# One more pair of contraction tiles by seven products in the key and value projections, another order of the first query block, and another order of the fold's splits

## The chip, the cores and the metric

The kernel runs on one core of a Trainium2 chip. The metric is the device time of one execution in microseconds (us). It is given as the median of the runs; beside it stands one execution that was profiled, with its span from the first to the last instruction. PE is the tensor engine, DVE the vector engine, ACT the scalar engine, and SP issues the transfers of the weights.

## The reference, cut to what matters

One encoder layer over 256 tokens of 2048 channels, in float32: a feed-forward half step, a mixer, attention over 256 memory tokens, a second feed-forward half step, and a last norm. The change lies in the attention:

```python
x = x + mem_cross_attention(rms_norm(x, xattn_norm), rms_norm(mem, mem_norm), w_q, w_kv, w_o)

def mem_cross_attention(h, mem_h, w_q, w_kv, w_o):      # 4 heads of 512
    q = (h @ w_q).reshape(b, s, 4, 512)
    kv = (mem_h @ w_kv).reshape(b, 256, 2, 4, 512)
    k, v = kv[:, :, 0], kv[:, :, 1]
    logits = jnp.einsum('bshd,bmhd->bhsm', q, k) * 512 ** -0.5
    p = jax.nn.softmax(logits, axis=-1)
    o = jnp.einsum('bhsm,bmhd->bshd', p, v).reshape(b, s, 2048)
    return o @ w_o
```

## The kernel before, in words

**Products in two parts.** Every float32 operand is split into a high part, which ACT casts, and a low part, which DVE gets as the difference to the high part. One product of two operands is then three matmuls: high by high, high by low, low by high. Weights come from HBM in units of 1 MB (two contraction tiles of 128 rows by 1024 columns) into one of three buffers `raw`; a unit's high and low parts are `wh` and `wl`. The units are numbered through the whole program; in the instruction orders below `wl185` belongs to unit 185. A profile's rows leave the numbers out.

**Plain units and units of 7.** A block (`block_s`) multiplies 256 rows of activations `xs` by 1024 columns of weights in 8 units. A plain unit is 8 products, 24 matmuls of 512 columns. In a unit of 7 (`split_seven`, `seven`) the two tiles of rows and the two of columns are taken as a 2 by 2 product with 7 products in place of 8, 21 matmuls. It needs sums of the weights and of the activations. DVE makes the weights' sums in `T` (three additions, L445), ACT casts the high parts of the sums (`wh`, two casts, L448) and of the raw columns (`xh`, L261), and DVE subtracts for `wl` (L449) and `xl` (L262). A plain unit has one ACT cast (L261) and one DVE subtraction (L262). The sums of the activations are made once for each pair of contraction tiles (`Sums.make`): an addition (L406) and four small ones (L413 to L418) on DVE, with a split of the results into `ye` and back into `xs` (L267 on ACT, L268 on DVE).

**Order.** `Stream` writes the work unit by unit: weights are split two units ahead of the unit that PE multiplies, and a raw buffer is loaded again once its unit is split. Splits of weights stand on ACT and DVE in the order in which they are written (`in_turn`), sums of activations among them (`among_weights`). `st.op(f, n)` puts other work behind the n-th next unit. A scheduler then sets each engine's order at build time; on the chip each engine runs its own instructions strictly in order.

**Buffers of the attention.** `T`, `xh` and `xl` have no tiles of their own here: they take turns in tiles of the attention stage that are free (`KV_HOMES`). In the key and value blocks `xh` and `xl` together have two tiles of one name, `att`. So a unit of 7 can cast its `xh` only when the previous unit of 7 has made its last product with the tile that is taken over.

**The stage.** Two query blocks (`w_q`), then key block 0, value block 0, key block 1, value block 1 (`w_kv`). The query blocks are units 182 to 189 and 190 to 197, the key and value blocks 198 to 229 in eights. Before the query blocks `fold` turns x by PE transposes into a PSUM tile of two banks, four pieces of 256 columns, and splits each piece into `xs` (`split_scaled`: ACT L230, then DVE L231). `mem_fold` does the same with the memory tokens, in place of x, once the second query block no longer needs those pairs. After a block its four extra products are combined (L530 to L535) and joined (L545). The queries and keys of a head are turned (L735); `logits` (L1273) with the softmax and `probs` follow a key block, `values` (L1312) a value block.

Before, the query blocks have the pairs 4 and 5 as units of 7, the key and value blocks the pairs 0 and 4.

Of the kernel before, what the change touches and what calls it, by code (L numbers as in the profile page):

```python
# [15 lines left out]
D = 2048  # L16
S = 256
# [3 lines left out]
NB = 512  # L21
# [9 lines left out]
G_FFN1, G_MIX, G_X, G_MEM, G_FFN2, G_PS, G_HN, G_BA, G_END = 0, 16, 32, 48, 64, 80, 88, 96, 100  # L31
# [62 lines left out]
def build(ctx, tc, I, out):  # L94
# [36 lines left out]
    def ptile(name):  # L131
        return psum.tile([P, 2, NB], F32, tag="ps", name=name)

    def four(ps):
        return ps.rearrange("p a (b c) -> p (a b) c", c=S)
# [3 lines left out]
    def uid(s):  # L139
        cnt[0] += 1  # L140
        return f"{s}{cnt[0]}"
# [42 lines left out]
    xs = main.tile([P, KT, 2, S], F32R, tag="xs", name="xs")  # L184
    ys = main.tile([P, KT, 2, S], F32R, tag="ys", name="ys")

    def gcol(i):
        return gains[:, i : i + 1]
# [4 lines left out]
    def f32(ap):  # L193
        return ap.bitcast(F32)
# [30 lines left out]
    def spread(ps, t, d):  # L225

        nc.tensor.matmul(ps[:, t * P : (t + 1) * P], ones, d, start=True, stop=True)

    def split_scaled(dst, kt, src, scale):
        hi = nc.scalar.activation(dst[:, kt, 0, :], src, AF.Copy, scale=scale)  # L230
        lo = nc.vector.scalar_tensor_tensor(  # L231
            out=dst[:, kt, 1, :], in0=src, scalar=scale, in1=f32(dst[:, kt, 0, :]),
            op0=ALU.mult, op1=ALU.subtract,
        )
        return hi, lo
# [16 lines left out]
    def among_weights(f):  # L252


        scalar, vector = behind_weights(f)
        latest["vector"] = vector
        if scalar is not None:
            latest["scalar"] = scalar
# [7 lines left out]
    def split(hi, lo, src):  # L266
        high = nc.scalar.copy(hi, src)  # L267
        return high, nc.vector.tensor_tensor(out=lo, in0=src, in1=f32(hi), op=ALU.subtract)  # L268
# [10 lines left out]
    diag, rows = {}, {}  # L279
# [301 lines left out]
    def wload(dst, w, k0, n, n0, cols=NB):  # L581
        nc.sync.dma_start(
            dst, w[k0 * P : (k0 + n) * P, n0 : n0 + cols].rearrange("(k p) n -> p k n", p=P)
        )
# [9 lines left out]
    def wwide(w, n0, k0=0, nk=KT):  # L594

        def src(k):
            def load(raw):
                raw = raw.rearrange("p (k n) -> p k n", n=2 * NB)
                if len(loaded) < 3:
                    for kk in range(2):  # L600
                        parts = (0, NB) if not loaded else (0,)
                        for c in parts:
                            n = 2 * NB // len(parts)
                            wload(raw[:, kk : kk + 1, c : c + n], w, k + kk, 1, n0 + c, n)
                else:
                    wload(raw, w, k, 2, n0, 2 * NB)
                next(first_loads, None)
                loaded.append(1)
            return load
        return [src(k0 + k) for k in range(0, nk, 2)]  # L610
# [51 lines left out]
    def x_cols(c, n):  # L662

        b = c // (2 * NB)
        return xrows[b][:, :, c - b * 2 * NB : c - b * 2 * NB + n]

    def x_chunk(c):
        v = ptile(uid("px"))[:, 0, :].rearrange("p (a b) -> p a b", a=2)
        k = 2 * c
        for j in range(2):  # L670
            for h in range(2):
                nc.tensor.transpose(
                    v[:, j, h * P : (h + 1) * P], x_cols((k + j) * P, P)[:, h], ident
                )
        for j in range(2):
            rows["parts", c, j] = split_scaled(xs, k + j, v[:, j, :], gcol(G_FFN1 + k + j))
        if c:
            latest["scalar"], latest["vector"] = rows["parts", c, 1]

# [60 lines left out]
    def fold(c, gain):  # L740

        v = four(ptile(uid("px")))
        x = x_cols(c * NB, NB)
        for j in range(4):
            for h in range(2):
                nc.tensor.transpose(  # L746
                    v[:, j, h * P : (h + 1) * P], x[:, h, j * P : (j + 1) * P], ident
                )
        def parts():
            for j in range(4):  # L750
                done = split_scaled(xs, 4 * c + j, v[:, j, :], gcol(gain + 4 * c + j))
            return done

        among_weights(parts) if c >= 2 else parts()
        for h in range(2):
            q = tmp.tile([P, NB], F32, tag="j", name=uid("j"))
            nc.scalar.activation(q, x[:, h], AF.Square, accum_out=ss[:, h, c : c + 1])
# [429 lines left out]
    def homes(of):  # L1187
        return lambda: scope.update(shared={tag: list(of[tag]) for tag in of})
# [7 lines left out]
    def xt(name, shape, dt=F32, tag=None, bufs=1):  # L1196
        t = whole_lines(scope["pool"], shape, dt, tag or name, uid(name), bufs)
        xa[name] = t
        return t
# [16 lines left out]
    def mem_fold(c):  # L1216

        v = four(ptile(uid("tm")))
        for j in range(4):
            for h in range(2):  # L1220
                nc.tensor.transpose(
                    v[:, j, h * P : (h + 1) * P],
                    xa[f"mem{h}"][:, c * NB + j * P : c * NB + (j + 1) * P], ident,
                )
        for j in range(4):
            split_scaled(xs, 4 * c + j, v[:, j, :], gcol(G_MEM + 4 * c + j))

    OUTPUT.make_sums((1, 4))
# [3 lines left out]
    for c in range(4):  # L1232
# [4 lines left out]
    w_q, w_kv, w_o = I["xattn_w_q"][0], I["xattn_w_kv"][0], I["xattn_w_o"][0]  # L1237


    q_sums, Q_ORDER = Sums("ye", xs, (4, 5), True, 2), ((0, 1, 2, 4, 3, 5, 6, 7),  # L1240
                                                        (0, 1, 4, 2, 5, 3, 6, 7))
    kv_sums, KV_ORDER = Sums("ye", xs, (0, 4), True, 2), (1, 5, 2, 0, 3, 6, 4, 7)
    held = {}

    def ev_Q(b):
        def evict(j, c):
            for h in range(2):
                nc.scalar.activation(c[:, h, :], c[:, h, :], AF.Copy, scale=Rcol[:, h : h + 1])
            held["Q", b, j] = c
        return evict  # L1250

    def turn_Q(b, j):
        k = 8 * b + 4 * j
        split(ys[:, k : k + 4, 0, :], ys[:, k : k + 4, 1, :], rows_turned(held["Q", b, j]))

    def turn_K(h):
        v = rows_turned(held["K", h])
        K = xa["K", h] = xt("K", [P, 4, 2, M], F32R, tag="kv", bufs=2)
        split(K[:, :, 0, :], K[:, :, 1, :], v)

    def ev_V(b):
        def evict(j, c):
            V = xa["V", 2 * b + j] = xt("V", [P, 2, 2, XHD], F32R, tag="kv", bufs=2)
            split(V[:, :, 0, :], V[:, :, 1, :], c)
        return evict
# [25 lines left out]
    def probs(h):  # L1291
        ps = ptile(uid("pt"))
        for mtile in range(2):
            for t in range(2):
                nc.tensor.transpose(
                    ps[:, mtile, t * P : (t + 1) * P], xa["P", h][:, t, mtile * P : (mtile + 1) * P], ident
                )
        if h % 2 == 0:
            xt("PT", [P, D], F32R)
        PT = xa["PT", h] = xa["PT"][:, h % 2 * 4 * S : (h % 2 + 1) * 4 * S].rearrange(  # L1300
            "p (m a s) -> p m a s", m=2, a=2
        )
        split(PT[:, :, 0, :], PT[:, :, 1, :], ps[:, :, :S])
# [11 lines left out]
                    )  # L1315
            split_pair(ys, 4 * h + 2 * p, ps[:, :, :S])

    for g, after in zip(q_sums.pairs, (2, 4)):
        st.op(lambda g=g: among_weights(lambda: q_sums.make(g)), after)
    for b in range(2):  # L1320
        block_s(wwide(w_q, b * 2 * NB), xs, q_sums, Q_ORDER[b], ev_Q(b))
        for j in (1, 0):
            st.op(lambda b=b, j=j: turn_Q(b, j), 1)
        if b == 0:
            for c, after in enumerate((5, 7, 6, 8)):
                st.op(lambda c=c: mem_fold(c), after)
    st.op(homes(KV_HOMES))
    for g, after in zip(kv_sums.pairs, (0, 2)):
        st.op(lambda g=g: among_weights(lambda: kv_sums.make(g)), after)
    for b in range(2):  # L1330
        block_s(wwide(w_kv, b * 2 * NB), xs, kv_sums, KV_ORDER, lambda j, c, b=b: held.__setitem__(
            ("K", 2 * b + j), c))
        for j in (1, 0):
            h = 2 * b + j
            st.op(lambda h=h: turn_K(h), 1)
        for h in (2 * b, 2 * b + 1):
            st.op(lambda h=h: logits(h), 2)
            st.op(lambda h=h: probs(h), 3)
        block_s(wwide(w_kv, D + b * 2 * NB), xs, kv_sums, KV_ORDER, ev_V(b))
        for h in (2 * b, 2 * b + 1):  # L1340
            st.op(lambda h=h: values(h), 1)
    st.op(homes(OUT_HOMES))
# [214 lines left out]
```

## Time and profile before

| | |
|---|---|
| median of 3 runs | 2091.51 us (2090.76 to 2091.64) |
| the profiled execution | 2093.45 us, span 2091.6 us |
| PE busy | 2075.2 us, 99% of the span |
| DVE, ACT busy | 1795.8 us (86%), 1134.2 us (54%) |
| read from HBM | 417.58 MB, 208 GB/s over the span |

The profiled execution is 1.94 us longer than the median; 1.85 us of it lie around the span. Matmuls overlap in the record: one lasts 390 ns from start to end, but the next starts earlier than that, so PE counts as busy while it is waiting for less than the overlap. A wait of PE is therefore best seen in the starts of its rows.

### The profile page before, as it was taken

What the parts mean: (1) busy time and instruction counts of PE and PEld (TensorE: products, weight loads), DVE (VectorE), ACT (ScalarE), POOL (GpSimd) and SP (SyncE); (2) the same over time, 40 slices, a digit from 0 to 9 for tenths busy, and PEclk for the clock granted to TensorE, in tenths of its full rate; (3) what the DMA queues carried; (4) which work ended last, traced back from release to release, by engine and by line L of the source; (5) the groups of instructions that cost most, each with busy time, mean ns of one, the idle gap of its engine ahead of it and who ended that gap; (6) DMA issues with size and microseconds to landing.
All of it is one profiled execution on the core that took longest, in us unless ns stands there. A gap on an engine that the chain in (4) does not pass through costs nothing.

```text
span 2091.6 us, 24183 instructions
## 1 busy us (share of the span) xinstructions
PE 2075.2 (99%) x9669; PEld 1728.6 (83%) x9669; DVE 1795.8 (86%) x1639; ACT 1134.2 (54%) x1118; POOL 14.2 (1%) x41
## 2 busy tenths in 40 slices
PE   9999999999999999999999999999999999999998
PEld 7888888888888888888788888888888888888886
DVE  7999899989998677688788777879998999989974
ACT  7655455644654555365665544556554556545544
POOL 0000000000000000000000000000000000000001
PEclk9999999999999999999999999999999999999999
DMA  7556666566656655467555555656576765676673
GB/s 263 201 196 228 240 221 207 194 223 237 226 195 239 215 181 192 152 198 264 198 185 185 174 182 174 222 189 220 181 241 209 243 207 187 224 239 223 209 255 118
DMA packets 131321, 435.94 MB, mean 208 GB/s; under 512 B 9860, under 2 KB 13544, under 8 KB 130824
## 3 DMA queue, kind: packets, MB, share of 16 engines
q1 hardware_dynamic: 131176, 434.38, 61.2%
q8 instruction: 76, 1.25, 0.2%
q14 instruction: 37, 0.30, 0.0%
q10 hardware_dynamic: 32, 0.01, 0.0%
HBM read 417.58 MB, written 16.78 MB: 208 GB/s over the span
## 4 chain that ended last, share of the span: by engine, by line
PE 93%; DVE 3%; ACT 1%; issue 1%; DMA 1%; SPq 0%; DVEq 0%; ACTq 0%
PE pt L344 53%; PE pt L468 25%; PE pa L329 6%; PE pe L344 3%; PE pb L344 2%; PE ph L735 1%; DVE wl L262 1%; DVE T L445 1%; DVE wl L449 1%; PE pl L1273 1%; PE pv L1312 1%; ACT wh L261 0%; PE px L746 0%; DVE xl L262 0%; DMA raw<-in_xattn_w_kv 0%
## 5 line engine op out<-in xcount | busy, mean ns | idle before, releaser
L262 DVE TENSOR_TENSOR wl<-raw,wh 128x2048 fp32r<-128x2048 f32 (+2 forms) x267 | 597.9, 2246 | 146.7 <-ACT wh L261 145.7
L344 PE MATMUL pt<-wh,xs 128*128 128x512 f32 x2112 | 677.9, 390 | 0.0
L261 ACT CAST wh<-raw 128x2048 fp32r<-128x2048 f32 (+2 forms) x267 | 500.3, 1879 | 289.4 <-PE pt L344 120.9
L344 PEld LDWEIGHTS pt<-wh,xs 128*128 128x128 f32 x2112 | 395.6, 188 | 81.0
L448 ACT CAST wh<-T 128x1024 fp32r<-128x1024 f32 x230 | 241.8, 1053 | 361.1 <-DVE T L445 355.0
L344 PE MATMUL pt<-wh,ys 128*128 128x512 f32 x1360 | 427.9, 390 | 0.0
L344 PE MATMUL pt<-wl,xs 128*128 128x512 f32 x1056 | 412.7, 391 | 0.0
L344 PEld LDWEIGHTS pt<-wh,ys 128*128 128x128 f32 x1360 | 254.9, 188 | 52.5
L344 PE MATMUL pt<-wl,ys 128*128 128x512 f32 x680 | 264.9, 390 | 0.0
L449 DVE TENSOR_TENSOR wl<-T,wh 128x2048 fp32r<-128x2048 f32 x115 | 262.6, 2283 | 1.2 <-ACT wh L448 0.5
L344 PEld LDWEIGHTS pt<-wl,xs 128*128 128x128 f32 x1056 | 198.4, 188 | 41.2 <-DVE wl L262 0.5
L262 DVE TENSOR_TENSOR xl<-raw,xh 128x1536 fp32r<-128x1536 f32 x115 | 201.3, 1751 | 18.9 <-ACT xh L261 17.3
L261 ACT CAST xh<-raw 128x1536 fp32r<-128x1536 f32 x115 | 170.1, 1479 | 32.3 <-PE pt L468 20.3
L445 DVE TENSOR_TENSOR T<-T,raw 128x512 f32<-128x512 f32 x230 | 158.7, 690 | 6.1
L344 PEld LDWEIGHTS pt<-wl,ys 128*128 128x128 f32 x680 | 127.7, 188 | 26.3
L468 PE MATMUL pt<-wh,xs 128*128 128x512 f32 x368 | 143.5, 390 | 0.7 <-ACT xs L267 0.7
L445 DVE TENSOR_TENSOR T<-raw 128x1024 f32<-128x1024 f32 x115 | 140.0, 1218 | 0.5
L468 PE MATMUL pt<-xh,xs 128*128 128x512 f32 x368 | 138.2, 391 | 0.1
L329 PE MATMUL pa<-xs,wh 128*128 128x512 f32 x384 | 135.0, 396 | 0.0
L468 PE MATMUL pt<-wh,xe 128*128 128x512 f32 x320 | 124.5, 389 | 0.0
L329 PE MATMUL pa<-xs,wl 128*128 128x256 f32 x384 | 106.6, 281 | 0.0
L329 PEld LDWEIGHTS pa<-xs,wh 128*128 128x128 f32 x384 | 71.7, 188 | 16.0 <-issue 0.3
(237 smaller groups left out, 2304.0 us busy)
## 6 DMA issues: line engine op xcount, KB each, us to landing
raw<-in_ffn_w_down SPq DMA_DIRECT2D x88, 1024.0 KB, 5.5
raw<-in_ffn_w_up SPq DMA_DIRECT2D x80, 1024.0 KB, 5.0
raw<-in_ffn_w_gate SPq DMA_DIRECT2D x77, 1024.0 KB, 5.2
raw<-in_w_in SPq DMA_DIRECT2D x32, 1024.0 KB, 5.2
raw<-in_xattn_w_kv SPq DMA_DIRECT2D x32, 1024.0 KB, 5.1
raw<-in_w_out SPq DMA_DIRECT2D x16, 1024.0 KB, 5.6
raw<-in_xattn_w_q SPq DMA_DIRECT2D x16, 1024.0 KB, 5.8
raw<-in_xattn_w_o SPq DMA_DIRECT2D x16, 1024.0 KB, 5.6
```

Of the source, the lines that this page charges most:

```text
L261: in_turn("scalar", lambda: nc.scalar.copy(hi, src))
L262: in_turn("vector", lambda: nc.vector.tensor_tensor(out=lo, in0=src, in1=f32(hi), op=ALU.subtract))
L329: nc.tensor.matmul(o, w, x, start=k == 0 and i == 0, stop=last and i == 1)
L344: nc.tensor.matmul(ps, a, w, start=first and i == 0, stop=last and i == 2)
L445: in_turn("vector", lambda: nc.vector.tensor_tensor(out=o, in0=a, in1=b, op=ALU.add))
L448: in_turn("scalar", lambda: nc.scalar.copy(th[:, c], t[:, c]))
L449: in_turn("vector", lambda: nc.vector.tensor_tensor(out=tl, in0=t, in1=f32(th), op=ALU.subtract))
L468: nc.tensor.matmul(banks[n], x, w, start=n in fresh and j == 0, stop=n in ends and j == 2)
L735: nc.tensor.transpose(v[:, i, h * P : (h + 1) * P], g[:, h, i * P : (i + 1) * P], ident)
L1273: nc.tensor.matmul(ps[:, t, :M], ys[:, 4 * h + d, a, tok], xa["K", h][:, d, b, :], start=i == 0, stop=i == 11,)
L1312: nc.tensor.matmul(ps[:, d, :S], xa["V", h][:, m, a, col], xa["PT", h][:, m, b, :], start=i == 0, stop=i == 5,)
```

## The change

1. The four pieces of a folded tile are split in the order 0, 2, 1, 3 in place of 0, 1, 2, 3 (`BY_BANKS`), so that neighbours lie in different PSUM banks; the first feed-forward's `x_chunk` puts its two pieces into two banks.
2. The first query block runs its pairs in natural order: the pairs 4 and 5, its units of 7, stand fifth and sixth (before: fourth and sixth). Their sums are made behind units 3 and 4 (before: 2 and 4).
3. The keys and values get a third pair of 7, pair 3. Key block 0 runs its pairs as 1, 5, 2, **0**, 6, **3**, **4**, 7 and the three other blocks as 1, 5, **0**, 2, **3**, 6, **4**, 7 (units of 7 bold; before: 1, 5, 2, **0**, 3, 6, **4**, 7 in all four). The last `mem_fold` comes one unit later. Pair 4's sums get a tile of their own, `ye2`.

```diff
+    BY_BANKS = (0, 2, 1, 3)
...
     def x_chunk(c):
-        v = ptile(uid("px"))[:, 0, :].rearrange("p (a b) -> p a b", a=2)
+        v = ptile(uid("px"))
...
-            rows["parts", c, j] = split_scaled(xs, k + j, v[:, j, :], gcol(G_FFN1 + k + j))
+            rows["parts", c, j] = split_scaled(xs, k + j, v[:, j, :S], gcol(G_FFN1 + k + j))
...
         def parts():
-            for j in range(4):
+            for j in BY_BANKS:
                 done = split_scaled(xs, 4 * c + j, v[:, j, :], gcol(gain + 4 * c + j))
...
-        for j in range(4):
+        for j in BY_BANKS:
             split_scaled(xs, 4 * c + j, v[:, j, :], gcol(G_MEM + 4 * c + j))
...
-    q_sums, Q_ORDER = Sums("ye", xs, (4, 5), True, 2), ((0, 1, 2, 4, 3, 5, 6, 7),
+    q_sums, Q_ORDER = Sums("ye", xs, (4, 5), True, 2), ((0, 1, 2, 3, 4, 5, 6, 7),
                                                         (0, 1, 4, 2, 5, 3, 6, 7))
-    kv_sums, KV_ORDER = Sums("ye", xs, (0, 4), True, 2), (1, 5, 2, 0, 3, 6, 4, 7)
+    kv_sums = Sums("ye", xs, (0, 3, 4), True, 2)
+    KV_ORDER = ((1, 5, 2, 0, 6, 3, 4, 7), (1, 5, 0, 2, 3, 6, 4, 7))
...
-    for g, after in zip(q_sums.pairs, (2, 4)):
+    for g, after in zip(q_sums.pairs, (3, 4)):
...
-            for c, after in enumerate((5, 7, 6, 8)):
+            for c, after in enumerate((5, 7, 6, 9)):
                 st.op(lambda c=c: mem_fold(c), after)
...
-    for g, after in zip(kv_sums.pairs, (0, 2)):
+    for g, after in zip(kv_sums.pairs, (0, 3, 4)):
...
-        block_s(wwide(w_kv, b * 2 * NB), xs, kv_sums, KV_ORDER, lambda j, c, b=b: held.__setitem__(
+        block_s(wwide(w_kv, b * 2 * NB), xs, kv_sums, KV_ORDER[b], lambda j, c, b=b: held.__setitem__(
...
-        block_s(wwide(w_kv, D + b * 2 * NB), xs, kv_sums, KV_ORDER, ev_V(b))
+        block_s(wwide(w_kv, D + b * 2 * NB), xs, kv_sums, KV_ORDER[1], ev_V(b))
```

The order of SP's transfers and of POOL's work is the same in both programs, and so is that of the other engines outside the attention. Lines behind the first edit are 3 or 4 higher: L262 is L265, L468 is L471. In the folds every ACT split of a tile but its first waits for the DVE split just ahead of it, before and after alike; only the pieces' numbers differ.

How the instructions move is shown at three places. First DVE in the first query block, from the end of the fold on. Before, unit 185 is the first unit of 7, with a plain unit between it and the second, 187:

```order
L445 TENSOR_TENSOR T185_7409<-raw185_7275 128x1024
L445 TENSOR_TENSOR T185_7409<-T185_7409,raw185_7275 128x512 x2
L262 TENSOR_TENSOR xl185_7413<-raw185_7275,xh185_7412 128x1536
L449 TENSOR_TENSOR wl185_7411<-T185_7409,wh185_7410 128x2048
L406 TENSOR_TENSOR j282_7460<-xs_107 128x512
L413 TENSOR_TENSOR j282_7460<-j282_7460 128x128
L414 TENSOR_TENSOR j282_7460<-j282_7460 128x128
L415 SCALAR_TENSOR_TENSOR j282_7460<-j282_7460 128x128
L268 TENSOR_TENSOR xs_107<-j282_7460,xs_107 128x128
L418 TENSOR_TENSOR j282_7460<-j282_7460 128x128
L262 TENSOR_TENSOR wl186_7471<-raw186_7305,wh186_7470 128x2048
L445 TENSOR_TENSOR T187_7508<-raw187_7339 128x1024
```

The same place after:

```order
L265 TENSOR_TENSOR wl185_7410<-raw185_7275,wh185_7409 128x2048
L448 TENSOR_TENSOR T186_7450<-raw186_7305 128x1024
L448 TENSOR_TENSOR T186_7450<-T186_7450,raw186_7305 128x512 x2
L265 TENSOR_TENSOR xl186_7454<-raw186_7305,xh186_7453 128x1536
L452 TENSOR_TENSOR wl186_7452<-T186_7450,wh186_7451 128x2048
L409 TENSOR_TENSOR j286_7498<-xs_107 128x512
L416 TENSOR_TENSOR j286_7498<-j286_7498 128x128
L417 TENSOR_TENSOR j286_7498<-j286_7498 128x128
L271 TENSOR_TENSOR xs_107<-j286_7498,xs_107 128x128
L418 SCALAR_TENSOR_TENSOR j286_7498<-j286_7498 128x128
L421 TENSOR_TENSOR j286_7498<-j286_7498 128x128
L448 TENSOR_TENSOR T187_7508<-raw187_7339 128x1024
```

The plain unit's subtraction stands first now, the two units of 7 (186, 187) follow each other, and the same instructions stand behind the fold in both.

Second, DVE at the end of key block 0. Before, unit 203 is plain and unit 204 is the next unit of 7 after 201:

```order
L262 TENSOR_TENSOR wl203_8219<-raw203_8089,wh203_8218 128x2048
L445 TENSOR_TENSOR T204_8247<-raw204_8152 128x1024
L268 TENSOR_TENSOR ye314_8074<-j320_8178,ye314_8074 128x384
L268 TENSOR_TENSOR ys_108<-ph318_8117,ys_108 128x4x256
L268 TENSOR_TENSOR ys_108<-ph319_8128,ys_108 128x4x256
L445 TENSOR_TENSOR T204_8247<-T204_8247,raw204_8152 128x512 x2
L262 TENSOR_TENSOR xl204_8251<-raw204_8152,xh204_8250 128x1536
L449 TENSOR_TENSOR wl204_8249<-T204_8247,wh204_8248 128x2048
```

After, units 203 and 204 are both of 7:

```order
L452 TENSOR_TENSOR wl203_8220<-T203_8218,wh203_8219 128x2048
L409 TENSOR_TENSOR j324_8257<-xs_107 128x512
L416 TENSOR_TENSOR j324_8257<-j324_8257 128x128
L417 TENSOR_TENSOR j324_8257<-j324_8257 128x128
L271 TENSOR_TENSOR xs_107<-j324_8257,xs_107 128x128
L418 SCALAR_TENSOR_TENSOR j324_8257<-j324_8257 128x128
L421 TENSOR_TENSOR j324_8257<-j324_8257 128x128
L448 TENSOR_TENSOR T204_8267<-raw204_8152 128x1024
L271 TENSOR_TENSOR ye2323_8256<-j324_8257,ye2323_8256 128x384
L448 TENSOR_TENSOR T204_8267<-T204_8267,raw204_8152 128x512 x2
L265 TENSOR_TENSOR xl204_8271<-raw204_8152,xh204_8270 128x1536
L452 TENSOR_TENSOR wl204_8269<-T204_8267,wh204_8268 128x2048
```

Pair 4's sums and the additions for `T204` stand behind `wl203` now, where `T204` stood ahead of unit 204's turn before.

Third, PE in value block 0, where the delayed products of one unit of 7 end and those of the next begin. Before (units 209 and 212; two plain stretches of unit 211 and six more products of 209 follow ahead of unit 212's first):

```order
L468 MATMUL pt341_8596<-xh209_8439,xs_107 128x512
L468 MATMUL pt341_8596<-xl209_8440,xs_107 128x512
L468 MATMUL pt341_8596<-xh209_8439,xs_107 128x512
L468 MATMUL pt341_8596<-wh209_8437,ye314_8074 128x512
L468 MATMUL pt341_8596<-wl209_8438,ye314_8074 128x512
L468 MATMUL pt341_8596<-wh209_8437,ye314_8074 128x512
L344 MATMUL pt325_8387<-wh211_8590,xs_107 128x512 x2
L344 MATMUL pt325_8387<-wl211_8591,xs_107 128x512
```

After (units 208 and 210; `pl336` are the logits of a head):

```order
L1277 MATMUL pl336_8527<-K329_8447,ys_108 128x256 x24
L471 MATMUL pt340_8577<-xh208_8400,xs_107 128x512
L471 MATMUL pt340_8577<-xl208_8401,xs_107 128x512
L471 MATMUL pt340_8577<-xh208_8400,xs_107 128x512
L471 MATMUL pt340_8577<-wh208_8398,ye313_8057 128x512
L471 MATMUL pt340_8577<-wl208_8399,ye313_8057 128x512
L471 MATMUL pt340_8577<-wh208_8398,ye313_8057 128x512
L471 MATMUL pt340_8577<-xh210_8565,xs_107 128x512
L471 MATMUL pt326_8412<-xh210_8565,xs_107 128x512
L471 MATMUL pt327_8413<-xh210_8565,ye313_8057 128x512
L471 MATMUL pt340_8577<-xl210_8566,xs_107 128x512
```

The first product of unit 210 with `xl` stands 8 matmuls behind the product with `xl208`, the last use of a tile that unit 210 takes over; before, unit 212's stood 22 behind the product with `xl209`.

## The prediction

> **What bounds the kernel now.** I read the page's span, shares and clock first, then PE's waits in groups, the timeline where PE waits, and last the groups of DVE and ACT. The page:
>
> ```profile
> span 2091.6 us, 24183 instructions
> PE 2075.2 (99%) x9669; PEld 1728.6 (83%) x9669; DVE 1795.8 (86%) x1639; ACT 1134.2 (54%) x1118; POOL 14.2 (1%) x41
> ...
> PEclk9999999999999999999999999999999999999999
> ```
>
> PE is the bound, at a full granted clock; DVE follows with 86%. The time is PE's matmuls plus what PE waits. A matmul's price comes from an undisturbed stretch of the timeline (start, duration, what, count):
>
> ```profile
> 1360.62 7.48 PE pt L468 x33
> ```
>
> 7.48 / 33 = 0.227 us. A plain unit is 24 × 0.227 = 5.44 us, a unit of 7 is 21 × 0.227 = 4.76. In the groups of PE's waits (total, count, longest) the attention shows little:
>
> ```profile
> PE tm L1221 <- DVE sg L545: 1.2, 1, 1.2
> ...
> PE pt L468 <- DVE wl L449: 0.8, 1, 0.8
> ...
> PE pt L468 <- ACT ye L267: 0.7, 2, 0.4
> ```
>
> Removing waits can win little here, and making some can lose more.
>
> **Fewer matmuls.** Pair 3 is of 7 in four blocks now (units 203, 210, 218, 226): 4 × 3 × 0.227 = **−2.7**.
>
> **The last fold of the memory, a unit later.** Its transposes wait for a join on DVE:
>
> ```profile
> 1097.37 1.09 PE L1221 MATMUL tm<-ident,mem 128*128 128x128 f32 x8 [1.18 <-DVE sg L545]
> ```
>
> One unit is 5.44 us, over four times the wait, so the join is done by then: 1.18 and some 0.1 of restart, **−1.3**. The ends are −1.3 and 0 (something else ends last); the delay is long, so I take −1.3.
>
> **The splits by banks.** In the fold ahead of the query blocks (idle time in brackets):
>
> ```profile
> 1008.75 0.47 ACT L230 ACTIVATE xs<-px,gains 128x256 fp32r<-128x256 f32 x1 [0.55 <-DVE xs L231]
> ...
> 1009.78 0.48 ACT L230 ACTIVATE xs<-px,gains 128x256 fp32r<-128x256 f32 x1 [0.56 <-DVE xs L231]
> ```
>
> The first row's piece lies in the bank of the piece before it; the second row crosses into the other bank. Both wait for DVE's last split, 0.55 and 0.56, and in the changed program each piece still waits for the one before. So **0**, for the memory's folds and the first feed-forward's chunks too. The ends: −3.6 (eight waits of this fold, worked out as a rival) and +0.1.
>
> [...]
>
> **The first query block in natural order.** The stretch from the fold's last splits to the second unit of 7:
>
> ```profile
> 1014.65 1.48 ACT L261 CAST xh<-raw 128x1536 fp32r<-128x1536 f32 x1
> 1015.19 1.22 DVE L445 TENSOR_TENSOR T<-raw 128x1024 f32<-128x1024 f32 x1
> 1017.77 1.75 DVE L262 TENSOR_TENSOR xl<-raw,xh 128x1536 fp32r<-128x1536 f32 x1
> ...
> 1018.64 0.61 PE L468 MATMUL pt<-xh,xs 128*128 128x512 f32 x2
> ...
> 1021.64 0.68 DVE L406 TENSOR_TENSOR j<-xs 128x512 f32<-128x512 f32 x1
> 1023.63 2.28 DVE L262 TENSOR_TENSOR wl<-raw,wh 128x2048 fp32r<-128x2048 f32 x1
> ...
> 1036.34 0.50 PE L468 MATMUL pt<-xh,ye 128*128 128x512 f32 x1 [0.36 <-ACT ye L267]
> 1036.67 0.39 PE L468 MATMUL pt<-xl,ye 128*128 128x512 f32 x1
> ...
> 1037.89 0.50 PE L344 MATMUL pt<-wl,xs 128*128 128x512 f32 x1
> ```
>
> The groups of the casts and subtractions (busy total and mean ns between the bars, then idle time before them):
>
> ```profile
> L261 ACT CAST wh<-raw 128x2048 fp32r<-128x2048 f32 x259 | 493.7, 1911 | 286.8 <-PE pt L344 120.9 <-issue 41.3 <-PE pa L329 32.7
> L262 DVE TENSOR_TENSOR wl<-raw,wh 128x2048 fp32r<-128x2048 f32 x259 | 590.3, 2286 | 145.0 <-ACT wh L261 144.2
> ...
> L448 ACT CAST wh<-T 128x1024 fp32r<-128x1024 f32 x230 | 241.8, 1053 | 361.1 <-DVE T L445 355.0 <-PE pt L468 3.0 <-PE pt L344 1.5
> L449 DVE TENSOR_TENSOR wl<-T,wh 128x2048 fp32r<-128x2048 f32 x115 | 262.6, 2283 | 1.2 <-ACT wh L448 0.5
> ```
>
> PE runs 63 matmuls between 1018.64 and 1037.89: 14.3 us of work in 19.25, so 4.9 are lost to DVE and ACT, which come out of the fold late. The set of instructions behind the fold stays the same. But DVE now begins with unit 185's plain `wl`, which needs an ACT cast of 1.91: 1014.65 + 1.91 = 1016.56, where before it began `T` at 1015.19, 1.37 later. The later sums still end the stretch, at a `ye` for which PE already waits (1036.34): **+1.5**. The ends: −4.9 (a plain unit first gives DVE the time it lacks, and the loss goes) and +3 (units 186 and 187 of 7 now follow each other, so `xl187` also waits for PE's last use of `xl186`). I take the value near the measured delay.
>
> **Units of 7 that stand closer.** This is the main term. `xh` and `xl` have one pair of tiles in the key and value blocks, so a unit of 7 starts its casts only after PE's last `xl` product of the previous one. Before, at units 201 and 204:
>
> ```profile
> 1127.99 0.39 PE L468 MATMUL pt<-xl,xs 128*128 128x512 f32 x1
> 1128.41 1.48 ACT L261 CAST xh<-raw 128x1536 fp32r<-128x1536 f32 x1 [8.24 <-PE pt L468]
> 1129.93 1.76 DVE L262 TENSOR_TENSOR xl<-raw,xh 128x1536 fp32r<-128x1536 f32 x1 [5.39 <-ACT xh L261]
> 1131.82 2.29 DVE L449 TENSOR_TENSOR wl<-T,wh 128x2048 fp32r<-128x2048 f32 x1
> ...
> 1132.98 0.39 PE L468 MATMUL pt<-xl,xs 128*128 128x512 f32 x1
> ...
> 1135.02 0.39 PE L468 MATMUL pt<-wl,xs 128*128 128x512 f32 x1
> ```
>
> From that last product's start (1127.99) `xl` is ready (1129.93 + 1.76) after 3.70 us and `wl` (1131.82 + 2.29) after 6.12. PE wants them after 4.99 and 7.03, 22 and 31 matmuls on. The chain is hidden with 1.3 and 0.9 us to spare. After the change, counted in PE's order:
>
> - Unit 203 (previous one 201): 15 matmuls to `xl`, 23 to `wl`: 3.41 and 5.22 of cover. Waits 3.70 − 3.41 = 0.3, then 6.12 − 5.22 − 0.3 = 0.6: 0.9.
> - Units 210 and 226 (previous 208, 224): 8 and 17 matmuls, 1.82 and 3.86. Waits 1.9, then 0.4: 2.3 each.
> - Unit 218 (previous 216): 15 and 24, 3.41 and 5.45. Waits 0.3 and 0.4: 0.7.
> - Units 212, 220, 228: over 40 matmuls, 9.1 us: no wait.
> - Unit 204 (previous 203, adjacent) is held by DVE's queue. Let X be the time at which `xl203` is ready. `wl203` ends at X + 2.4. Pair 4's sums stand next, 1023.63 − 1021.64 = 2.0 for the like before: T204 begins at X + 4.4. The first addition and a cast behind it (1.22 + 1.05) bring `wh204` at X + 6.7; from the start of `T` to the end of `xl` it took 1017.77 + 1.75 − 1015.19 = 4.3 before, and `ye`'s split between adds 0.5: `xl204` at X + 9.2. PE, after its wait for `wl203`, wants `wh204` at X + 5.2 (1.5 of waiting) and `xl204` a matmul later, X + 6.95 (2.2), then `wl204` 0.2: 3.9.
>
> In value block 0 a delayed product of unit 208 takes a PSUM tile from head 0's logits, with only the other head's 24 logits to cover the softmax:
>
> ```profile
> 1159.85 5.79 PE L1273 MATMUL pl<-K,ys 128*128 128x256 f32 x47
> ...
> 1162.79 0.69 DVE L1279 TENSOR_REDUCE nm<-pl 128x2 f32<-128x512 f32 x1 [3.36 <-PE pl L1273]
> ...
> 1165.88 0.20 ACT L1283 ACTIVATION_READ_ACCUMULATOR P<-pl,nm 128x1 f32 x1
> ```
>
> The softmax lasts from 1162.79 to 1165.88 + 0.20 = 1166.08, while PE is through its logits at 1159.85 + 47 × 0.12 = 1165.5: 0.6 more.
>
> After a wait PE also starts slower: 1036.67 − 1036.34 = 0.33 instead of 0.227. For some 12 waits that is +1.3.
>
> The waits add 0.9 + 3.9 = **+4.8** in key block 0, 2.3 + 0.6 = **+2.9** in value block 0, **+0.7** in key block 1, **+2.3** in value block 1, and **+1.3** for the restarts. The ends: nothing (the chain finds more cover, a rival) and DVE's full added work (below). I take the chain as it was measured, with the cover counted.
>
> **DVE's work.** A unit of 7 costs DVE, by these rows, 1.22 + 2 × 0.69 + 1.75 + 2.28 = 6.6, a plain one 2.29:
>
> ```profile
> L445 DVE TENSOR_TENSOR T<-T,raw 128x512 f32<-128x512 f32 x230 | 158.7, 690 | 6.1
> ...
> 1085.00:1325.00 240.00, 238.82 (x1190) 202.36 (x1189) 187.15 (x183) 123.44 (x130) 0.00 (x0) 1.00 0.52 176
> ```
>
> Four more are 17.4, and pair 3's sums about 2.6 (2.0 and a `ye` split): 20 us. The second row gives 240 us of the key and value blocks: PE's 238.82, its loads, DVE's 187.15, ACT's 123.44. DVE has 53 us free, so 20 fit on the whole, only not within the two units by which splits lead. The order of SP's transfers is unchanged; a raw buffer comes free at most about 2 us later, in the shadow of the two units (10.9 us) of lead. POOL has nothing here.
>
> **Sum:** −2.7 − 1.3 + 0 + 1.5 + 4.8 + 2.9 + 0.7 + 2.3 + 1.3 = **+9.5**. The profiled execution took 2093.45 and would become 2103.0; it lies 1.94 above the median of 2091.51, so the median becomes **2101.0**.
>
> **Rivals.**
> 1. *The waits stay hidden* (the other sign). If ACT and DVE get through a unit's chain in what PE's 8 to 24 matmuls cover, only −2.7 − 1.3 is left: 2087.5, and 2082.6 if the query block's 4.9 go as well. It decides where the chain to `xl` is under 1.8 us; the measured 3.70 speaks against it. 0.08.
> 2. *The banks do matter.* The eight pieces' pitch is 1009.78 − 1008.75 = 1.03; without the wait it is about half, 8 × 0.45 = 3.6 less, and the query block's loss of 4.9 nearly goes. In place of +1.5 stands −4.8: 2094.7. Against it: equal waits within a bank and across. 0.04.
> 3. *DVE becomes the bound* in the key and value blocks, so all 20 us show: 20 − 4 = +16, 2107.5. Against it: 53 us free. 0.06.
> 4. *Nearly no change.* The waits are half as long, since delays overlap (a late PE gives DVE time), and the query block costs nothing: some 2093. Against it: most gates are PE's own products, and move with PE. 0.08.
>
> **How the numbers follow.** My forecast has 0.74. About 0.2%, 4.2 us, is what a measurement of this kernel can tell from no change. Rival 1 is split, 0.05 faster (under 2087.3) and 0.03 same; rivals 2 and 4 are same, and 0.01 of the forecast's edge. That makes faster 0.05, same 0.16, slower 0.79. The forecast's own range is 2095 to 2106: the query block's ends and a third of the waits. The range 2090.5 to 2108 takes in the rivals 2, 3 and 4, and leaves out rival 1 and the far tails.
>
> **What the changed profile would show.** PE's wait for `sg` at the last fold gone; the waits in the folds still 0.55; the first query block still with some 5 us of gaps. New PE waits, for DVE's `xl` and `wl` and ACT's `wh`, near 1125 to 1140 (about 5 us), 1165 to 1180 (3), in key block 1 (under 1) and in value block 1 (2). I am wrong if these blocks show no gaps, if the waits hang on DMA, or if DVE runs through the key and value blocks without idle time.

## The result, and the profile after

The changed kernel takes 2103.86 us in the median of 4 runs (2101.90 to 2105.41), the kernel before 2091.57 (2090.76 to 2091.86). The ratio is 1.0059, 95% interval 1.0041 to 1.0076: slower by 12.3 us. The forecast was +9.5, 2101.0.

The profiled executions differ by less: 2093.45 before, 2101.90 after, +8.45. The page of the changed kernel, the lines that answer to those of before:

```profile
span 2100.0 us, 24195 instructions
PE 2076.2 (99%) x9657; PEld 1724.6 (82%) x9657; DVE 1814.5 (86%) x1662; ACT 1141.5 (54%) x1128; POOL 14.2 (1%) x41
...
PEclk9999999999999999999999999999999999999999
```

PE has 12 matmuls fewer, DVE 18.7 us more work. The shares hardly move, and whoever reads only the profile's page does not find the loss. PE's waits from the first query block to value block 1 show it (total, count, longest):

```profile
PE pt L471 <- DVE xl L265: 5.5, 6, 1.8
PE pt L471 <- ACT xh L264: 1.3, 2, 0.6
PE pt L471 <- ACT wh L451: 1.2, 1, 1.2
PE pt L471 <- DVE wl L452: 1.1, 2, 0.8
...
PE pt L471 <- ACT P L1287: 0.5, 1, 0.5
```

The largest stand in key block 0, one matmul apart, ahead of unit 204:

```profile
1126.62 0.50 PE L471 MATMUL pt<-xl,xs 128*128 128x512 f32 x1 [0.19 <-DVE xl L265]
...
1129.05 0.51 PE L471 MATMUL pt<-wl,xs 128*128 128x512 f32 x1 [0.32 <-DVE wl L452]
...
1131.72 0.48 PE L471 MATMUL pt<-xh,ye 128*128 128x512 f32 x1
1133.43 0.49 PE L471 MATMUL pt<-wh,xs 128*128 128x512 f32 x1 [1.23 <-ACT wh L451]
1135.76 0.50 PE L471 MATMUL pt<-xl,xs 128*128 128x512 f32 x1 [1.84 <-DVE xl L265]
```

From start to start, less one matmul of 0.227, the last two are 1.48 and 2.11 us. (The bracket gives less, since it counts only the time in which the record shows PE idle.) In value block 0, unit 210 waits for both halves of its chain, 0.80 and 1.00 us:

```profile
1174.22 0.72 PE L471 MATMUL pt<-xh,xs 128*128 128x512 f32 x2 [0.63 <-ACT xh L264]
...
1176.01 0.50 PE L471 MATMUL pt<-xl,xs 128*128 128x512 f32 x1 [0.83 <-DVE xl L265]
```

Counting by the same matmuls in both traces, the profiled difference splits up like this:

| stretch | before | after | difference |
|---|---|---|---|
| first 400 matmuls | 89.76 | 88.37 | −1.39 |
| 100 matmuls of the first query block | 27.54 | 28.92 | +1.38 |
| memory's folds to value block 1 | 206.26 | 215.11 | +8.85 |
| the next 600 matmuls | 127.27 | 126.89 | −0.38 |

The rest of the trace is equal to within 0.1 us; the sum is +8.46.

### The profile page after: what moved, and what is told of

Read it like the earlier page. It is cut to its first block, busy times and chain, and to the rows that moved or that the text cites. A ratio compares the mean times of both kernels' runs of the same rounds, so it can differ in the third digit from the quotient of the medians.

```text
span 2100.0 us, 24195 instructions
## 1 busy us (share of the span) xinstructions
PE 2076.2 (99%) x9657; PEld 1724.6 (82%) x9657; DVE 1814.5 (86%) x1662; ACT 1141.5 (54%) x1128; POOL 14.2 (1%) x41
## 4 chain that ended last, share of the span: by engine, by line
PE 93%; DVE 4%; ACT 1%; issue 1%; DMA 0%; SPq 0%; DVEq 0%; ACTq 0%
PE pt L347 52%; PE pt L471 25%; PE pa L332 6%; PE pe L347 3%; PE pb L347 2%; PE ph L738 1%; DVE xl L265 1%; DVE wl L452 1%; DVE T L448 1%; DVE wl L265 1%; PE pv L1316 1%; PE px L749 0%; PE pl L1277 0%; ACT xh L264 0%; PE pp L969 0%
## 5 line engine op out<-in xcount | busy, mean ns | idle before, releaser
L265 DVE TENSOR_TENSOR wl<-raw,wh 128x2048 fp32r<-128x2048 f32 (+2 forms) x263 | 589.0, 2246 | 140.0 <-ACT wh L264 139.2
L347 PE MATMUL pt<-wh,xs 128*128 128x512 f32 x2048 | 660.1, 390 | 0.7 <-ACT xs L233 0.5
L264 ACT CAST wh<-raw 128x2048 fp32r<-128x2048 f32 (+2 forms) x263 | 492.5, 1878 | 273.6 <-PE pt L347 115.3
L451 ACT CAST wh<-T 128x1024 fp32r<-128x1024 f32 x238 | 250.2, 1053 | 369.7 <-DVE T L448 356.8
L347 PEld LDWEIGHTS pt<-wh,xs 128*128 128x128 f32 x2048 | 383.4, 188 | 80.2 <-ACT xs L233 0.7
L347 PE MATMUL pt<-wl,xs 128*128 128x512 f32 x1024 | 399.9, 391 | 0.4 <-DVE wl L265 0.4
L452 DVE TENSOR_TENSOR wl<-T,wh 128x2048 fp32r<-128x2048 f32 x119 | 271.7, 2283 | 1.2 <-ACT wh L451 0.5
L265 DVE TENSOR_TENSOR xl<-raw,xh 128x1536 fp32r<-128x1536 f32 x119 | 208.3, 1751 | 7.3 <-ACT xh L264 6.3
L471 PE MATMUL pt<-wh,xs 128*128 128x512 f32 x384 | 149.8, 390 | 2.1 <-ACT wh L451 1.2
L471 PE MATMUL pt<-xh,xs 128*128 128x512 f32 x384 | 144.8, 392 | 1.9 <-ACT xh L264 1.3
L471 PE MATMUL pt<-wh,xe 128*128 128x512 f32 x320 | 124.5, 389 | 0.0
L471 PEld LDWEIGHTS pt<-xh,xs 128*128 128x128 f32 x384 | 71.9, 188 | 19.3 <-ACT xh L264 3.5
```

The source lines that it names most:

```text
L264: in_turn("scalar", lambda: nc.scalar.copy(hi, src))
L265: in_turn("vector", lambda: nc.vector.tensor_tensor(out=lo, in0=src, in1=f32(hi), op=ALU.subtract))
L347: nc.tensor.matmul(ps, a, w, start=first and i == 0, stop=last and i == 2)
L451: in_turn("scalar", lambda: nc.scalar.copy(th[:, c], t[:, c]))
L452: in_turn("vector", lambda: nc.vector.tensor_tensor(out=tl, in0=t, in1=f32(th), op=ALU.subtract))
L471: nc.tensor.matmul(banks[n], x, w, start=n in fresh and j == 0, stop=n in ends and j == 2)
```

## The experiments

The theory: the third pair puts units of 7 so close that ACT's and DVE's chain for one is not done when PE wants it. It names two causes: the shared tiles of `xh` and `xl`, and DVE's queue ahead of unit 204. Each ratio below is against the kernel before on the same chip. The rivals: the other edits are at fault; DVE's 20 us of added work are the bound; the difference between profile and median is something else again.

**The changed kernel once more.** No edit.

> The changed kernel once more, to see how far its executions lie apart and whether the waits are the same each time. If the added time is waits of PE on ACT and DVE (the theory), the groups of PE's waits in the key and value blocks come out as in the first profile, some 10 us without the restarts, and the ratio to the kernel before is 1.004 to 1.007. If the median's +12.3 beside the profile's +8.4 comes from the granted clock (rival), the executions differ by 2 to 4 us and the clock by 0.001 to 0.002, with the same waits.

2103.75 us (2103.29 to 2105.72), ratio 1.006 (1.0047 to 1.0072). The waits are the same to 0.1 us. But the span of this profiled execution is 3.9 us longer than that of the first one, and here is where most of it lies, in the timeline of PE behind the two long waits:

```profile
1137.10 0.80 PE L471 MATMUL pt<-xl,xs 128*128 128x512 f32 x1 [1.83 <-DVE xl L265]
1137.69 0.63 PE L471 MATMUL pt<-xh,xs 128*128 128x512 f32 x1
1138.12 0.63 PE L471 MATMUL pt<-xl,xs 128*128 128x512 f32 x1
...
1142.38 0.63 PE L471 MATMUL pt<-wl,ye 128*128 128x512 f32 x1
1142.81 0.52 PE L471 MATMUL pt<-wh,ye 128*128 128x512 f32 x1
```

The starts lie 0.43 us apart instead of 0.227. A view by windows (window, length, busy time of PE, PE's loads, DVE, ACT and POOL, then granted clock, DMA share, GB/s) has the same stretch, first of the first profile, then of this one:

```profile
1137.00:1143.00 6.00, 6.00 (x27) 4.72 (x26) 5.96 (x5) 4.21 (x3) 0.00 (x0) 1.00 0.75 238
```
```profile
1137.00:1143.00 6.00, 5.90 (x14) 4.66 (x15) 6.00 (x4) 3.06 (x2) 0.00 (x0) 0.50 0.60 185
```

Half the clock (0.50 for 1.00), half the matmuls (14 for 27): some 2.6 us lost. Ahead of this stretch, from 10 to 1131 us, and behind it, from 1143 to 2080, the granted clock is 1.00. The other 1.3 us are a wait for the join at a memory fold (1.0) and the start (0.4).

**The splits by banks alone.** The first of the three edits on the kernel before.

```diff
-            for j in range(4):
+            for j in BY_BANKS:
                 done = split_scaled(xs, 4 * c + j, v[:, j, :], gcol(gain + 4 * c + j))
...
-        v = ptile(uid("px"))[:, 0, :].rearrange("p (a b) -> p a b", a=2)
+        v = ptile(uid("px"))
```

> The kernel before with the splits by banks alone (folds, and the first feed-forward's chunks over two banks). The prediction gave this 0. The profile of the changed kernel has everything 1.4 us earlier from the first feed-forward's start on, so this theory expects -1.4 (ratio 0.9993), all of it in the first 10 us, and the same 0.55 us waits inside the folds of the query blocks. If neighbouring banks let the splits of those folds overlap, the stretch from the fold to 1038 us is shorter by up to 3.6 us and the ratio about 0.998.

2091.01 us, ratio 1.0000 (0.9991 to 1.0009): no difference, where −1.4 was expected. In the fold ahead of the query blocks every split waits as before:

```profile
1007.31 0.47 ACT L232 ACTIVATE xs<-px,gains 128x256 fp32r<-128x256 f32 x1 [0.55 <-DVE xs L233]
1008.34 0.48 ACT L232 ACTIVATE xs<-px,gains 128x256 fp32r<-128x256 f32 x1 [0.55 <-DVE xs L233]
```

These two cross from one bank to the other, and DVE's last split still has to end first. Whether the 1.4 us at the start are the edit's is not shown: the first 400 matmuls took 88.4 to 88.9 us in the nine profiles with it, and 89.8, 89.3 and 88.8 in the three without. A gain of half a microsecond would fit these and the medians alike.

**Without the third pair.** The changed kernel with the key and value blocks as they were.

```diff
-    kv_sums = Sums("ye", xs, (0, 3, 4), True, 2)
-    KV_ORDER = ((1, 5, 2, 0, 6, 3, 4, 7), (1, 5, 0, 2, 3, 6, 4, 7))
+    kv_sums, KV_ORDER = Sums("ye", xs, (0, 4), True, 2), (1, 5, 2, 0, 3, 6, 4, 7)
...
-    for g, after in zip(kv_sums.pairs, (0, 3, 4)):
+    for g, after in zip(kv_sums.pairs, (0, 2)):
...
```

> The changed kernel without its third pair of 7 (key and value blocks as before; splits by banks, natural order of the first query block and the later fold of the memory are kept). If the loss is the closer units of 7 (the theory), what is left is -1.4 at the start, +0.7 in the first query block and -1.3 at the fold of the memory: -2.0, ratio 0.9990. If the loss comes from the other edits, or from how they move DVE's work, the ratio stays above 1.002.

2092.96 us, ratio 1.0006 (0.9997 to 1.0016): the loss is gone but for some 1.4 us, where −2.0 was expected. The first query block's +1.4 is there; the gains at the start and at the fold do not show in the median.

**The third pair alone.** The last edit, without the memory's later fold, on the kernel before.

```diff
-    kv_sums, KV_ORDER = Sums("ye", xs, (0, 4), True, 2), (1, 5, 2, 0, 3, 6, 4, 7)
+    kv_sums = Sums("ye", xs, (0, 3, 4), True, 2)
+    KV_ORDER = ((1, 5, 2, 0, 6, 3, 4, 7), (1, 5, 0, 2, 3, 6, 4, 7))
...
-    for g, after in zip(kv_sums.pairs, (0, 2)):
+    for g, after in zip(kv_sums.pairs, (0, 3, 4)):
...
```

> The kernel before with the third pair of 7 alone. The theory: -2.7 of matmuls and +12 of waits with their restarts, +9.4, ratio 1.0045, with PE's waits for xl, wl and wh in the four key and value blocks as in the changed kernel (about 5, 3.6, 0.8 and 2.8 us). The rival, that the changed order of the first query block or the later memory fold pushes DVE's work into the key blocks, expects clearly fewer waits, a ratio of 1.002 or less.

2102.53 us, ratio 1.0051 (1.0039 to 1.0064): +11.0, with the changed kernel's waits in place (0.35, 0.48, 1.48 and 2.11 us in key block 0). The other edits are not at fault for this part; what is missing to the changed kernel's +12.3 is about the query block's 1.4. Behind the two long waits the half clock is here too, for a shorter time (0.52 granted from 1136 to 1139 us, 0.91 from 1139 to 1142).

**Other tiles for the middle unit of 7.** The changed kernel with one assignment.

```diff
-    KV_HOMES = {"T": [("sg", D, 2)], "xh": [("att", 3 * NB, 2)], "xl": [("att", 3 * NB, 2)]}
+    KV_HOMES = {"T": [("sg", D, 2)],
+                "xh": [("att", 3 * NB, 2), ("kv", D, 2), ("att", 3 * NB, 2)],
+                "xl": [("att", 3 * NB, 2), ("kv", D, 2), ("att", 3 * NB, 2)]}
```

> The changed kernel with one edit: in the key and value blocks the middle unit of 7 of a block puts its xh and xl into the two tiles kv, which are free there, so that no unit of 7 waits for the xl products of the one before it. The work of all engines stays the same. If the waits come from the tiles that the closer units share (the theory), those of units 203, 210, 218 and 226 go, some 6.5 us with their restarts; the wait of unit 204 behind pair 4's sums on DVE (3.6) and that for the softmax (0.7) may stay. Some 2097 us, ratio 1.0025. If DVE's 20 us of added work are the cause (rival), the waits stay within 1 us of the changed kernel's total, ratio 1.005 or more.

2097.09 us, ratio 1.0025 (1.0016 to 1.0034), the time that the theory gave: 6.7 us below the changed kernel, with the same work on every engine. The waits of the units 203 and 218 are gone, unit 226 waits 0.50 us for the softmax where its two waits for `xh` and `xl` were 1.81, and the shared tiles are shown to be a cause. That the time fits so well is in part luck, since two departures cancel. Unit 204's waits, which were expected to stay, fell from 3.59 to 1.43 us: DVE begins pair 4's sums at 1125.92 here, at 1128.91 in the changed kernel. And in value block 0, where 1.80 were to go, another wait stands in the place of the old ones, 2.38 us from start to start less one matmul:

```profile
1165.35 1.47 ACT L264 CAST xh<-raw 128x1536 fp32r<-128x1536 f32 x1 [11.67 <-PE pl L1279]
...
1168.74 1.28 ACT L1289 ACT_TABLE_LOAD   x1
```
```profile
1171.11 0.50 PE L471 MATMUL pt<-xh,xs 128*128 128x512 f32 x1 [2.22 <-ACT P L1289]
```

The tiles `kv` hold the keys until head 1's logits have read them, so unit 210's casts start only then, and the softmax queues behind them on ACT.

**Two units of 7 in key block 0.** The changed kernel; pair 3 of that block is multiplied as a plain unit. The pair's sums have by then replaced a part of its activations, so the keys of two heads are not what the reference computes; the instructions and their order are what the time needs.

```diff
         block_s(wwide(w_kv, b * 2 * NB), xs, kv_sums, KV_ORDER[b], lambda j, c, b=b: held.__setitem__(
-            ("K", 2 * b + j), c))
+            ("K", 2 * b + j), c), sevens=None if b else (0, 4))
```

> The changed kernel with pair 3 of key block 0 done as a plain unit (24 matmuls in place of 21), all else the same. The theory: the 4.9 us of waits and restarts of that block go and 0.7 of matmuls comes back, so -4.2 on the first profile's span of 2100.0. If the two long waits ahead of unit 204 (1.5 and 2.1 us, one matmul apart) also set off the stretch at half the granted clock that followed them in two of three profiles, the executions here have no such stretch at 1131 to 1143 us, lie closer together and are 5 to 7 us below the changed kernel's median: 2097 to 2099, ratio 1.003. If that stretch has nothing to do with the waits, it is seen here too and the median falls by 4 only.

2097.46 us, ratio 1.0029 (1.0018 to 1.0040). The profile is 4.3 us below the first one of the changed kernel, as the waits and the matmuls make it, and has the full clock in this block (1.00 granted from 1114 to 1143 us). The executions do not lie closer together, as was expected (2096.60 to 2099.76). The median is 6.4 us lower; the 2 us between fit the half clock that followed the long waits in two other profiles (0.50 for 6.8 us, 0.52 for 3). That the waits bring it on, this comparison supports and doesn't prove.

**Covered, with earlier sums.** The splits by banks and the third pair on the kernel before, with the tiles of the run before last, and:

```diff
-    for g, after in zip(kv_sums.pairs, (0, 3, 4)):
+    for g, after in zip(kv_sums.pairs, (0, 2, 3)):
...
```

> The kernel before with the splits by banks and the third pair, with the tiles of the run named e5_tiles and the sums of pairs 3 and 4 made one unit earlier, so that they stand ahead of unit 203's additions on DVE; the first query block and the memory's folds stay as before. If the chain of casts is all that costs (the theory), it is covered everywhere and the -2.7 of matmuls shows, with -0.5 at the start and 0.8 for the softmax: 2089, ratio 0.9988. If DVE is the bound in these blocks (rival), ratio above 1.002.

2096.15 us, ratio 1.0021 (1.0012 to 1.0030): a miss, by 7 us, and above the 1.002 that the rival named. DVE's row for 1114 to 1134 us, before the change and here:

```profile
1114.00:1134.00 20.00, 20.00 (x98) 16.82 (x97) 14.37 (x14) 9.93 (x10) 0.00 (x0) 1.00 0.37 117
```
```profile
1114.00:1134.00 20.00, 18.21 (x86) 14.42 (x85) 19.38 (x21) 10.97 (x12) 0.00 (x0) 1.00 0.35 110
```

DVE went from 14.37 to 19.38 of 20 us and pauses no more from 1118.8 on. With the tiles out of the way it is itself the bound here, and PE waits for `xl203` and `xl204`, 0.7 and 1.4 us. That is the rival's part of the miss. The larger one is not DVE's work: in value block 0 the wait of the run with other tiles has only another name (2.15 us from start to start less one matmul), since the tiles `kv` are not free there, and the half clock follows it (0.66 granted from 1170 to 1175 us, with matmuls 0.43 us apart):

```profile
1170.62 0.51 PE L470 MATMUL pt<-xl,xs 128*128 128x512 f32 x1 [1.98 <-DVE xl L264]
...
1171.78 0.63 PE L470 MATMUL pt<-xh,ye 128*128 128x512 f32 x1
```

**The query block's order alone.** The second edit on the kernel before.

```diff
-    q_sums, Q_ORDER = Sums("ye", xs, (4, 5), True, 2), ((0, 1, 2, 4, 3, 5, 6, 7),
+    q_sums, Q_ORDER = Sums("ye", xs, (4, 5), True, 2), ((0, 1, 2, 3, 4, 5, 6, 7),
...
-    for g, after in zip(q_sums.pairs, (2, 4)):
+    for g, after in zip(q_sums.pairs, (3, 4)):
```

> The kernel before with the natural order of the first query block alone. The prediction's step: +1.5. The profiles of the kernels with and without this order give +1.4 between the fold and the end of that block, without a change of the granted clock, and a wait for xl of 1.8 us that could set off a stretch at half clock (0.78 was granted at 1030 to 1036 us in one of them): 2093 to 2094.5, ratio 1.0007 to 1.0014. If the natural order gives DVE the time it lacked (the other end of the prediction's bounds), 2087.

2092.49 us, ratio 1.0006 (0.9997 to 1.0016). By itself the interval can't tell this from no change, but the same 100 matmuls can: 28.9 us in all seven profiled executions with this order, 27.5 to 27.6 in the five without. Two of the seven have a half-clock stretch there (0.54 granted from 1033.0 to 1036.5 us) and are no longer for it, since PE waits for DVE in this block anyway. In the first profile of the changed kernel DVE starts behind the fold and PE's last wait of this stretch ends as follows:

```profile
1015.15 2.29 DVE L265 TENSOR_TENSOR wl<-raw,wh 128x2048 fp32r<-128x2048 f32 x1 [1.31 <-ACT wh L264]
```
```profile
1037.12 0.50 PE L347 MATMUL pt<-wl,xs 128*128 128x512 f32 x1 [0.42 <-DVE wl L265]
```

This execution is 1.44 us ahead of the one before the change when it comes to this block, so DVE starts 1.40 us later. From 1015.15 to that last wait it has no gap, so it is DVE's queue that PE waits for (1.79 us at most, for `xl187`), and not the tiles that the units 186 and 187 share.

**Key block 0 spaced.** The changed kernel; a plain unit stands between the units 202 and 204.

```diff
-    KV_ORDER = ((1, 5, 2, 0, 6, 3, 4, 7), (1, 5, 0, 2, 3, 6, 4, 7))
+    KV_ORDER = ((1, 5, 0, 2, 3, 6, 4, 7), (1, 5, 0, 2, 3, 6, 4, 7))
...
-    for g, after in zip(kv_sums.pairs, (0, 3, 4)):
+    for g, after in zip(kv_sums.pairs, (0, 2, 4)):
```

> The changed kernel with key block 0 in the order of the three other blocks, 1, 5, 0, 2, 3, 6, 4, 7, so that a plain unit stands between its second and third unit of 7 (202 and 204); pair 3's sums are made a unit earlier. The work is the same. If the two long waits of that block come from the neighbouring units 203 and 204 with pair 4's sums between them on DVE (the theory), key block 0 behaves like key block 1: 0.4 and 0.25 us of waits in place of 4.4, no stretch at half clock behind them, and the median is 4.5 to 6 us below the changed kernel's: 2098 to 2099.5, ratio 1.0035. If DVE simply has too much work in this block, with the folds of the memory and the sums of three pairs in it (rival), waits of 2 us and more stay there.

2099.70 us, ratio 1.0038 (1.0026 to 1.0051): 4.1 us less. The two long waits are gone, and with them, in the profiled execution, the half clock (1.00 granted from 1114 to 1143 us), so the neighbouring units were the larger cause. But 1.8 us of waits remain in the block, 0.65 were expected, and one is new:

```profile
1119.94 0.50 PE L471 MATMUL pt<-wh,xs 128*128 128x512 f32 x1 [0.99 <-DVE ys L271]
...
1133.19 0.50 PE L471 MATMUL pt<-xl,xs 128*128 128x512 f32 x1 [0.46 <-DVE xl L265]
```

The split of the turned queries (`ys`) is late now. In this block DVE has too much to do within the lead, in both orders tried: here the rival holds in part.

**The third pair in the second half alone.** The kernel before with the splits by banks; pair 3 is of 7 in key block 1 and value block 1, with the tiles `kv` for the middle unit.

```diff
+    KV_SEVENS = ((0, 4), (0, 3, 4))
...
+        if b:
+            st.op(homes(KV3_HOMES))
+            st.op(lambda: among_weights(lambda: kv_sums.make(3)), 1)
...
```

> The kernel before with the splits by banks, and pair 3 of 7 in key block 1 and value block 1 alone, the middle unit's xh and xl in the tiles kv; everything before key block 1 is as before. By the runs so far: -0.5 at the start, -0.7 in key block 1 with its chain fully covered, and in value block 1 -0.7 against a wait for the softmax of 0.5 and two restarts: -1.0 to -1.7 in all, 2090 to 2090.6, ratio 0.9993 to 0.9996, so at most half of what can be told from no change. If DVE's work is what costs, it is above 1.000 here too, with waits in key block 1.

2090.93 us, ratio 0.9998 (0.9989 to 1.0007). Key block 1 shows no wait, value block 1 the 0.5 for the softmax and 0.33 for DVE. The median lies 0.3 us above the expected range, and no difference to the kernel before can be measured; none of these versions beats that kernel clearly.

## Why the prediction was right, step by step

- *Fewer matmuls, −2.7.* Right: 9657 in place of 9669.
- *Units of 7 that stand closer.* The mechanism and nearly every wait came as worked out. Units 203 and 204: 0.36, 0.48, 1.48 and 2.11 us, forecast 0.3, 0.6, 1.5 and 2.2 (0.2 more was forecast for `wl204` and did not show). Unit 210: 0.80 + 1.00, forecast 1.9; unit 226: 0.81 + 1.00; unit 218: 0.35, forecast 0.3. The waits for `wl` of these three: 0.25 each, forecast 0.4. The softmax: 0.66, forecast 0.6. Two waits of 0.33 for DVE, one in each value block, were not in the forecast. With restarts the waits are 12.1 us in the first profile; the forecast's terms make 12.0.
- *The first query block, +1.5.* Right in size: +1.38, and +1.4 with that edit alone. DVE starts later by about the forecast delay, but the stretch ends at a plain unit's `wl` and not at `ye`, so that the loss is as large as the delay is in part luck. The stretch read for the prediction holds 64 matmuls, not 63, so 4.7 us were lost in it before.
- *The splits by banks, 0.* Right, by the same 0.55 us waits and the medians. What the pieces wait for is the split ahead of them, in whichever bank: 0.55 us within a bank and 0.56 across before, 0.55 across with the edit alone. In the fold ahead of the query blocks neither of these two profiles shows two splits of one tile side by side.
- *The last fold of the memory, −1.3.* Wrong. The step read a wait of one profiled execution as the kernel's. It is 1.34 and 1.03 us in two of six profiled executions with the old place of the fold, and 1.0 and twice 0.2 in three of six with the new one. In one execution with the later fold the wait is thus as long as before, so the delay does not remove it; what brings it on in some executions is not shown. The step ought to have been near 0. The sum also took that wait off twice: as a gain, and within the 1.94 us by which this execution lies above the median. (These 1.94 lie inside the span, not around it: time and span differ by 1.7 to 1.9 us in every profile.)
- *DVE is not the bound.* Right for the 240 us as a whole, where DVE is busy for 196.99 us after the change, and since moving tiles alone took 6.7 us off with equal work; too simple for key block 0, where DVE has no gap left once the tiles are out of the way, and for the first query block.
- *The restart, +1.3.* Nearly right for what it names: 0.11 us each, for 15 waits in place of 12, 1.65. The sum lacks a cost that the prediction did not see: behind the longest waits the clock is halved in some executions (0.50 granted for 6.8 us in the second one of the changed kernel). The median's 12.3 us are the profiles' 8.45, and 1.9 by which before's profiled execution lay above its median, and 2.0 by which the first profile of the changed kernel, without a half-clock stretch, lay below its own.

So the forecast of 2101.0 was 2.9 us low: a gain of 1.3 that isn't there, and 1.5 to 2.6 us of half clock, an estimate from the 2.6 us lost in a stretch of 6.8 us and from the shorter one, of about half that length. That most executions have it is not shown; two of three profiles with these waits do.

## What to carry to other kernels

Before a unit is traded for one with fewer matmuls and more preparation, count from the trace the cover between the last use of its buffers and its own first use, in matmuls, and lay the chain of casts against it; 12 matmuls (2.7 us) were bought here for 12 us of waits. Freeing one resource moves the wait to the next (tiles, then the softmax's queue, then DVE itself), so a gain has to be reckoned to the second bound. A wait seen once in one profiled execution is not yet a term of the sum. And waits that come close together can cost more than their sum: in the second execution 2.6 us more, with 0.50 of the clock granted behind them.

## What was not expected of the hardware

Behind waits of PE that are each no longer than 2.2 us, the granted clock was halved in some executions. After 1.48 and 2.11 us of waiting with one matmul between them, it was 0.50 for 6.8 us in one profile (13 matmuls at 0.43 us, 2.6 us lost), half for a shorter time in another (the third pair alone, 0.52 from 1136 to 1139 us), and 1.00 in a third of the same order of work. After the query block's waits, 1.79 and 0.94 us in the first profile, 0.54 was granted from 1033.0 to 1036.5 us in two profiles (one is that of the kernel without the third pair, the row below, the other that with other tiles), and 1.00 in three others with this order (the changed kernel twice, and with key block 0 spaced). After the single wait of 2.15 us in value block 0 of the covered version, 0.66 was granted from 1170 to 1175 us.

```profile
1033.00:1036.50 3.50, 3.12 (x7) 1.90 (x8) 3.36 (x7) 3.47 (x10) 0.00 (x0) 0.54 0.73 269
```

Here are the stretch ahead of the half clock and the half clock itself in the second execution, and then the same work in the first, which came to it 1.34 us earlier:

```profile
1132.84:1136.25 3.41, 1.20 (x4) 0.37 (x2) 3.38 (x5) 2.04 (x3) 0.00 (x0) 1.00 0.00 0
...
1136.27:1143.08 6.81, 5.98 (x14) 4.74 (x15) 6.81 (x4) 3.79 (x3) 0.00 (x0) 0.50 0.55 165
```
```profile
1131.50:1134.91 3.41, 1.20 (x4) 0.37 (x2) 3.38 (x5) 2.04 (x3) 0.00 (x0) 1.00 0.00 0
1134.93:1141.74 6.81, 5.98 (x25) 4.72 (x26) 6.81 (x4) 5.03 (x5) 0.00 (x0) 1.00 0.56 164
```

PE was busy for 1.20 of 3.41 us in both, with the same loads, DVE and ACT beside it; 0.50 of the clock was granted behind this in the one and 1.00 in the other, 14 matmuls against 25 in 6.81 us. So the waits alone do not decide which executions are hit. What decides it is not shown, and no run was made to test it.
